# Small loads queued behind the diagonals, two sums of squares on VectorE, and the tail of one modulation block on TensorE

## The chip, the core and the metric

The kernel runs on one core of a Trainium2 chip. The core has TensorE (PE, with its weight loads shown apart as PEld), VectorE (DVE), ScalarE (ACT), GpSimd (POOL) and SyncE (SP), and sixteen DMA engines that they share. Each engine works through its own instructions strictly in order; between engines, semaphores make one wait for another. The metric is device time in microseconds (us) from launch to end. Before the change it is 2052.8 us, the median of three runs (2052.47 to 2053.01).

## What is computed

Three transformer layers, one sequence of 512 rows, width 1024, all in 32-bit floating point. The change lies in the beginning of the first layer:

```python
c_act = jax.nn.silu(c)
mod = jnp.einsum('bd,de->be', c_act, w_ada[l]) + b_ada[l]          # 6 x 1024 columns
sh1, sc1, g1, sh2, sc2, g2 = [m[:, None, :] for m in jnp.split(mod, N_ADA, axis=-1)]
h = rmsnorm(x, norm_mix_g[l]) * (1.0 + sc1) + sh1
proj = jnp.einsum('bsd,de->bse', h, w_in[l])
u_f, q, k, v = jnp.split(proj, split_cols, axis=-1)
q = rmsnorm(q.reshape(B, S, N_KV_HEADS, Q_PER_KV, HEAD_DIM), q_norm_g[l])
k = rmsnorm(k.reshape(B, S, N_KV_HEADS, HEAD_DIM), k_norm_g[l])
y_f = fourier_mix(u_f, w_fourier[l], b_fourier[l])
y_a = windowed_gqa(q, k, v, rel_bias, sink[l])                     # rel_bias: T5 bias table
mixed = jnp.einsum('bse,ed->bsd', jnp.concatenate([y_f, y_a], axis=-1), w_out[l])
x = x + g1 * mixed
```

A mixture of 16 experts follows in the same layer, then two more layers with other attention forms.

## The kernel before

**Phases.** `phase_a` makes everything quoted above; the expert phase and four more phases follow. The work is staged as one stream of 1 MB weight chunks (`wraw`, 128 x 2048 values), which SP loads in a fixed order; a chunk's load waits until its buffer is free. The first ten chunks take turns between a pool of three buffers and the two of `wp`; from then on there are the two buffers of `wp` alone, so a load is issued when the chunk two places earlier has been read.

**Modulation.** The 6144 columns of `mod` are worked in twelve blocks of 512, two chunks (halves) each. For a block, DVE adds up `acc[p, n] = sum over k of ca[p, k] * w[p, k, n]` in eight steps (`sums`, L656 and L658, for the first four blocks; `mod`, L612 and L614, for the others), and PE then sums over the partitions with a matrix of ones: into four columns (`columns`, L584) or, where the result is wanted as a row on all partitions (blocks 4, 5, 10, 11), as one 512-wide product (L619). Those four blocks start from a row of `b_ada`, which POOL loads into `acc` (L596) after clearing it (L594). The order of chunks is: block 2, block 0, first half of q, block 3, block 1, second half of q, block 4 (both halves), kv, block 5 (both halves), u (first), blocks 6 to 11 among u (second) and the attention.

**Start.** `load_x` brings the four row chunks of x. For each, ACT squares and sums (`ssq`, L444), `rstd` makes the reciprocal root on ACT and DVE, and POOL writes a diagonal matrix with it (`diags`, L694). PE multiplies x with the diagonals (`turn`, L674), which transposes and normalises in one go; `modulate` (L681 to L685) applies scale `a1` and shift `sh` and splits the result into a high and a low part, `hT_hi` and `hT_lo`. Weights are split likewise, `whi` on ACT (L403) and `wlo` on DVE (L404), and every product is three matmuls (`mm3`, L413 to L415).

**Then** come q (`proj_m`, into `qn`), kv (L736 copies the result out), the constants of the Fourier part (`fourier_mats`, L913), the sums of squares of q and k (`qss`, L741 to L743, which need both q and kv), their `rstd` over 40 columns, u (`pieces("u")`, `proj_s`), the scaled k and q (L767, L774) with their transposes (L777), the Fourier part, and attention in four blocks.

**Small loads** go through POOL's queue: the T5 table (`t5_table`: `c_t`, `tab`, then `t5scr`, which goes through DRAM and comes back as eight `bias` loads in `t5_bias`), `row_sink`, and `wf`, `c_cd`, `c_sd` for the Fourier part. Loads that are not pinned may be placed anywhere by the scheduler.

**Order.** A scheduler sets the order of each engine's instructions when the kernel is built, from data dependencies and its own estimates; an instruction given to `pin` keeps its place in program order among the pinned ones. What stands in a row on an engine is therefore fixed before the run.

Of the kernel before, what the change touches and what calls it, by code (L numbers as in the profile page):

```python
# [11 lines left out]
F32 = mybir.dt.float32  # L12
F32R = mybir.dt.float32r
BF16 = mybir.dt.bfloat16
# [3 lines left out]
OP = mybir.AluOpType  # L18
# [5 lines left out]
D = 1024  # L24
# [269 lines left out]
class Kernel:  # L294
# [262 lines left out]
    def phase_a(self, moe, pre):  # L557
        nc, tc, sp = self.nc, self.tc, self.sp
        with ExitStack() as es:
# [3 lines left out]
            p = self.pool(ea, "a_p")  # L563
# [5 lines left out]
            ones = pb.tile([128, 128], F32, name="ones")  # L569
# [12 lines left out]
            def columns(acc, pm, first=True, last=True):  # L582
                for j in range(4):
                    nc.tensor.matmul(pm[:, j:j + 1], acc[:, j * 128:j * 128 + 128], ones[:, :1],  # L584
                                     start=(j == 0 and first), stop=(j == 3 and last))
# [53 lines left out]
            pq = self.pool(e3, "a_q", side="right")  # L639
            pa = self.pool(e1, "a_ada", side="right")  # L640
# [2 lines left out]
            sh, a1, bg = (pa.tile([128, 8], F32, name=n) for n in ("sh", "a1", "bg"))  # L643
            nc.vector.scalar_tensor_tensor(bg, vc("ada", 8), 1.0, vc("mix", 0), op0=OP.add, op1=OP.mult)

            def sums(blk):
                acc = pb.tile([128, 512], F32, name="acc", bufs=2)
                for h in range(2):
                    w, _ = self.raw("ada")
                    if h == 1 and blk == 2:  # L650
                        self.load_x()
                    for k in range(4):
                        ck = ca[:, 4 * h + k:4 * h + k + 1]
                        wk = w[:, k * 512:(k + 1) * 512]
                        if h + k == 0:
                            nc.vector.tensor_scalar(acc, wk, ck, None, op0=OP.mult)  # L656
                        else:
                            nc.vector.scalar_tensor_tensor(acc, wk, ck, acc, op0=OP.mult, op1=OP.add)  # L658
                return acc

            def put(blk, pm):
                sl = slice(blk % 2 * 4, blk % 2 * 4 + 4)
                if blk < 2:
                    nc.vector.tensor_tensor(sh[:, sl], pm[:, :4], vc("ada", 4 * blk, 4), op=OP.add)
                else:
                    nc.vector.tensor_tensor(a1[:, sl], pm[:, :4], vc("mix", 4 * blk - 8, 4), op=OP.mult)
                    nc.vector.tensor_tensor(a1[:, sl], a1[:, sl], bg[:, sl], op=OP.add)

            diags = []

            def turn(k):
                pt = self.mm()
                for c in range(4):
                    nc.tensor.matmul(pt[:, c * 128:(c + 1) * 128], self.x[:, c, k * 128:(k + 1) * 128],  # L674
                                     diags[c], start=True, stop=True)
                return pt

            def modulate(k, pt):
                t = pa.tile([128, 512], F32, name="hx", bufs=2)
                if k % 2:  # L680
                    nc.scalar.activation(t, pt, AF.Identity, scale=a1[:, k:k + 1], bias=sh[:, k:k + 1])  # L681
                else:
                    nc.vector.tensor_scalar(t, pt, a1[:, k:k + 1], sh[:, k:k + 1], op0=OP.mult, op1=OP.add)
                nc.scalar.copy(hT[0][:, k], t)
                nc.vector.tensor_tensor(hT[1][:, k], t, hT[0][:, k].bitcast(F32), op=OP.subtract)  # L685

            acc = sums(2)
            pm = self.av()
            columns(acc, pm)
            put(2, pm)  # L690
            for c in range(4):
                rr = self.rstd(self.ssq(self.x[:, c]), 1, D)
                diags.append(pa.tile([128, 128], F32, name=f"diag{c}"))
                nc.gpsimd.tensor_scalar(diags[-1], self.ident, rr, -0.5, op0=OP.mult, op1=OP.mult)  # L694
            pts = [turn(k) for k in range(4)]
            scr = self.t5_table(pq)
            acc = sums(0)
            pm = self.av()
            columns(acc, pm)
            put(0, pm)  # L700
            for k in range(4):
                modulate(k, pts[k])

            def third(i):
                if i == 0:
                    pts[:] = [turn(k) for k in range(4, 7)]

            def second(i):
                if i == 0:
                    accs = [sums(3), sums(1)]  # L710
                    pm = self.mm()
                    for j in range(2):
                        columns(accs[j], pm[:, 4 * j:4 * j + 4], j == 0, j == 1)
                    put(3, pm)
                    put(1, pm[:, 4:8])
                    for k in range(4, 8):
                        modulate(k, pts[k - 4] if k < 7 else turn(k))
                fill(FILL[i], self.mm)
# [4 lines left out]
                        banks=[self.av] * 2 + [self.tp] * 2)  # L723
            e1.close()
            p = self.pool(ea, "a_p2")
            sink = self.row_load(p, "sink", 8)
            kv = p.tile([128, 4, 256], F32, name="kv")
            qz = p.tile([128, 4, 2, 512], F32, name="qz")
            nc.gpsimd.memset(qz[64:, :, 0, :], 0.0)
# [2 lines left out]
            with ExitStack() as e2:  # L732
# [6 lines left out]
                for c in range(4):  # L739
                    sq = self.nrm.tile([128, D], F32, name="xn", tag="xn")  # L740
# [6 lines left out]
                                               op0=OP.mult, op1=OP.mult)  # L747

                d = 0
                for j in range(2):  # L750
                    for w in self.pieces("u", 128):
                        ps = self.mm()
# [128 lines left out]
    def t5_table(self, tmp):  # L881

        nc = self.nc
        t5 = self.const_load(tmp, "t5", 33)
        tab = tmp.tile([33, 8], F32, name="tab")
        nc.vector.memset(tab, 1.0)
        nc.gpsimd.dma_start(tab[:32], self.ap["rel_bias"])
        ps = self.tp()
        self.pin(nc.tensor.matmul(ps[:8], tab, t5[:33], start=True, stop=True))
        v = tmp.tile([8, 512], F32, name="t5v")  # L890
        self.pin(nc.scalar.copy(v, ps[:8]))
        scr = self.dram.tile([8, 16, 512], F32, name="t5scr")
        self.pin(nc.gpsimd.dma_start(scr, v[:, None, :].to_broadcast([8, 16, 512])))
        return scr
# [9 lines left out]
    def fourier_mats(self, p, tmp):  # L904

        nc = self.nc
        wf = tmp.tile([64, 8, 64], F32, name="wf")
        nc.gpsimd.dma_start(wf, self.ap["w_fourier"].rearrange("g c d -> c g d"))
        mats = []
        for n in ("cd", "sd"):  # L910
            cd = self.const_load(tmp, n, 64)
            ps = self.tp()
            self.pin(nc.tensor.matmul(ps, cd[:64], wf.rearrange("p g d -> p (g d)"), start=True, stop=True))  # L913
            m = p.tile([128, 4, 128], F32, name="m_" + n)
            nc.gpsimd.memset(m, 0.0)
            p4 = ps.rearrange("p (j g d) -> p j g d", j=4, g=2)
            nc.scalar.copy(m[:64, :, :64], p4[:64, :, 0])
            nc.vector.tensor_copy(m[64:, :, 64:], p4[64:, :, 1])
            mats.append(m)
        return mats  # L920
# [1057 lines left out]
```

## Time and profile before

| | |
|---|---|
| median of three runs | 2052.8 us |
| the profiled execution, its own time | 2050.99 us |
| its span, first to last instruction | 2049.2 us |
| PE busy / DVE busy / ACT busy / POOL busy | 95% / 67% / 52% / 6% of the span |
| chain of work that ended last | PE 66%, DVE 10%, issue 6%, ACT 4% |
| phase A | about the first 245 us of the span |

The busy shares are averages over phases with different limits. In phase A the stretches of 20 us tell more: they show each engine's busy time, PE's granted clock and what the DMA engines moved.

### The profile page before, as it was taken

To read this page: it belongs to the slowest core of one execution; us is meant where nothing else is said; L and a number is where in the kernel's file an instruction comes from. 1 tells how busy PE (TensorE), PEld (TensorE's weight loads), DVE (VectorE), ACT (ScalarE), POOL (GpSimd) and SP (SyncE) were. 2 spreads that over 40 slices of the span, in tenths; PEclk is the share of its full clock that TensorE was granted. 3 is DMA by queue.
4 is the path that set the end of the run, shared out by engine and by line. 5 is a ranking of instruction groups with operands and counts; after the bars stand their busy time and mean duration, and the time that the engine had idled before them with its cause. 6 is when DMAs were issued, how large, how long until landed. Compare 5 with 4: busy or idle time off the path is not lost.

```text
span 2049.2 us, 24617 instructions
## 1 busy us (share of the span) xinstructions
PE 1939.1 (95%) x9147; PEld 1532.6 (75%) x9147; DVE 1363.5 (67%) x2294; ACT 1058.4 (52%) x1831; POOL 133.2 (6%) x132
## 2 busy tenths in 40 slices
PE   5999789999999998999999999999999989999998
PEld 4777567677676676877778888887887778888886
DVE  7885689999898998438665624554447775624554
ACT  3444377878777775346454423433345664423432
POOL 3004100000000201000110000002000020000001
PEclk9999889999999999999999999999999999999999
DMA  9635559999999983220222222222322032222221
GB/s 294 249 141 194 230 215 420 402 394 370 417 375 394 405 336 121 103 72 11 97 90 103 78 98 103 89 92 71 122 73 73 31 114 103 77 98 103 99 82 57
DMA packets 53805, 358.30 MB, mean 175 GB/s; under 512 B 6566, under 2 KB 7134, under 8 KB 13876
## 3 DMA queue, kind: packets, MB, share of 16 engines
q1 hardware_dynamic: 48148, 338.60, 43.1%
q0 software_dynamic: 5536, 18.12, 3.1%
q8 instruction: 72, 1.18, 0.2%
q14 instruction: 49, 0.40, 0.1%
HBM read 353.28 MB, written 4.46 MB: 175 GB/s over the span
## 4 chain that ended last, share of the span: by engine, by line
PE 66%; DVE 10%; issue 6%; ACT 4%; POOL 0%; DMA 0%; DVEq 0%; ACTq 0%; POOLq 0%
PE mm L413 12%; PE mm L414 12%; PE mm L415 12%; PE mm L281 11%; DVE wlo L281 5%; PE tp L413 2%; PE tp L414 2%; PE tp L415 2%; PE av L414 2%; PE av L415 2%; PE av L413 2%; ACT whi L281 2%; PE mm L1381 1%; PE tp L281 1%; PE av L281 1%
## 5 line engine op out<-in xcount | busy, mean ns | idle before, releaser
L404 DVE TENSOR_TENSOR wlo<-wraw,whi 128x1024 fp32r<-128x1024 f32 (+2 forms) x209 | 250.1, 1199 | 395.1 <-ACT whi L403 395.1
L281 DVE TENSOR_TENSOR wlo<-wraw,whi 128x1024 fp32r<-128x1024 f32 x336 | 392.7, 1217 | 31.2 <-ACT whi L281 28.7
L403 ACT CAST whi<-wraw 128x1024 fp32r<-128x1024 f32 (+2 forms) x209 | 214.2, 1029 | 326.4 <-PE mm L414 149.1
L413 PE MATMUL mm<-hT_hi,whi 128*128 128x512 f32 (+1 forms) x960 | 376.0, 393 | 0.2 <-DVE sba L1706 0.2
L415 PE MATMUL mm<-hT_hi,wlo 128*128 128x512 f32 (+1 forms) x960 | 373.5, 389 | 1.8 <-DVE wlo L404 1.8
L414 PE MATMUL mm<-hT_lo,whi 128*128 128x512 f32 (+1 forms) x960 | 374.3, 390 | 0.6 <-DVE hT_lo L419 0.6
L281 ACT CAST whi<-wraw 128x1024 fp32r<-128x1024 f32 x336 | 331.3, 1054 | 19.6 <-PE mm L281 17.4
L415 PEld LDWEIGHTS mm<-hT_hi,wlo 128*128 128x128 f32 x960 | 182.2, 190 | 43.2 <-DVE wlo L404 2.0
L413 PEld LDWEIGHTS mm<-hT_hi,whi 128*128 128x128 f32 x960 | 182.3, 190 | 41.3 <-ACT xn L742 0.8
L414 PEld LDWEIGHTS mm<-hT_lo,whi 128*128 128x128 f32 x960 | 182.1, 190 | 40.9 <-DVE hT_lo L419 1.4
L281 PE MATMUL mm<-whi,xs 128*128 128x512 f32 x448 | 186.6, 416 | 0.6 <-DVE xs L281 0.6
L281 PE MATMUL mm<-wlo,xs 128*128 128x512 f32 x448 | 181.0, 404 | 4.7 <-DVE wlo L281 4.7
L281 PEld LDWEIGHTS mm<-wlo,xs 128*128 128x128 f32 x448 | 85.4, 191 | 35.0 <-DVE wlo L281 16.5
L281 PEld LDWEIGHTS mm<-whi,xs 128*128 128x128 f32 x448 | 85.5, 191 | 21.4 <-ACT whi L281 1.9
L414 PE MATMUL mm<-wlo,hT_hi 128*128 128x512 f32 (+2 forms) x256 | 98.1, 385 | 1.2 <-DVE wlo L404 1.2
L413 PE MATMUL mm<-whi,hT_hi 128*128 128x512 f32 (+2 forms) x256 | 98.5, 388 | 0.8 <-ACT whi L403 0.8
L415 PE MATMUL mm<-whi,hT_lo 128*128 128x512 f32 (+2 forms) x256 | 97.3, 381 | 0.6 <-DVE hT_lo L419 0.6
L281 PE MATMUL mm<-whi,act 128*128 128x512 f32 x224 | 96.5, 431 | 0.0
L281 PE MATMUL mm<-wlo,act 128*128 128x512 f32 x224 | 90.4, 404 | 2.3 <-DVE wlo L281 2.3
L418 ACT CAST aT_hi<-cv 128x512 fp32r<-128x512 f32 x44 | 27.3, 621 | 116.9 <-DVE cv L1887 116.9
L1886 ACT ACTIVATE cv<-cv 128x512 f32<-128x512 f32 x44 | 27.8, 632 | 89.4 <-DVE cv L1883 89.4
L414 PE MATMUL av<-wlo,aT_hi 128*128 128x512 f32 x176 | 69.2, 393 | 0.0
(513 smaller groups left out, 3368.7 us busy)
## 6 DMA issues: line engine op xcount, KB each, us to landing
wraw<-in_wts SPq DMA_DIRECT2D x310, 1024.0 KB, 7.2
wraw<-in_wts SPq DMA_DIRECT2D x8, 768.0 KB, 4.2
x<-in_x SPq DMA_DIRECT2D x4, 512.0 KB, 12.3
out<-x SPq DMA_DIRECT2D x4, 512.0 KB, 2.6
wraw<-in_wts SPq DMA_DIRECT2D x2, 832.0 KB, 4.6
bias<-t5scr POOLq DMA_DIRECT2D x8, 192.0 KB, 9.5
hd<-xn POOLq DMA_DIRECT2D x3, 512.0 KB, 2.9
mod<-md POOLq DMA_DIRECT2D x1, 1024.0 KB, 10.5
```

What stands on the lines that cost most here:

```text
L281: ins = op(*a, **k)
L403: i1 = nc.scalar.copy(hi[:, :n], t[:, a:a + n])
L404: i2 = nc.vector.tensor_tensor(lo[:, :n], t[:, a:a + n], hi[:, :n].bitcast(F32), op=OP.subtract)
L413: mm(ps, a[0], b[0], start=start, stop=False)
L414: mm(ps, a[0], b[1], start=False, stop=False)
L415: mm(ps, a[1], b[0], start=False, stop=stop)
L418: self.nc.scalar.copy(hi, src)
L1381: nc.tensor.matmul(ps[:, :W], lhs[:, i * 128:(i + 1) * 128], rhs[:, :W], start=True, stop=True)
L1886: nc.scalar.activation(u[0], u[0], AF.Silu)
```

## The change

Four edits. (1) Loads: `c_t` and `tab` (now made after the second modulation block), `wf`, `c_cd`, `c_sd` and `row_sink` are pinned, and so are the four diagonals, so that these loads come after the diagonals in POOL's queue. (2) Chunks 1 and 3 of x are squared and summed on DVE with one tensor_tensor_reduce each; chunks 0 and 2 stay on ACT. (3) The last two of the eight steps of block 0 leave DVE: PE multiplies the chunk with the two columns of `ca` (one row of 512, in the bank `side`), ACT copies that row out, and four more one-column products add it to `pm`. (4) `t5_table` is called after `modulate` instead of before `sums(0)`.

```diff
-            def sums(blk):
+            def sums(blk, aside=None):
...
-                        if h + k == 0:
+                        if aside is not None and 4 * h + k > 5:
+                            nc.tensor.matmul(aside[:1], ck, wk, start=(k == 2), stop=(k == 3))
+                        elif h + k == 0:
                             nc.vector.tensor_scalar(acc, wk, ck, None, op0=OP.mult)
...
             for c in range(4):
-                rr = self.rstd(self.ssq(self.x[:, c]), 1, D)
+                if c % 2:
+                    ssq = sp.tile([128, 1], F32, name="ssq", tag="ssq")
+                    nc.vector.tensor_tensor_reduce(pa.tile([128, D], BF16, name="sq"), self.x[:, c], self.x[:, c], 1.0, 0.0,
+                                                   op0=OP.mult, op1=OP.add, accum_out=ssq)
+                else:
+                    ssq = self.ssq(self.x[:, c])
+                rr = self.rstd(ssq, 1, D)
                 diags.append(pa.tile([128, 128], F32, name=f"diag{c}"))
-                nc.gpsimd.tensor_scalar(diags[-1], self.ident, rr, -0.5, op0=OP.mult, op1=OP.mult)
+                self.pin(nc.gpsimd.tensor_scalar(diags[-1], self.ident, rr, -0.5, op0=OP.mult, op1=OP.mult))
             pts = [turn(k) for k in range(4)]
-            scr = self.t5_table(pq)
-            acc = sums(0)
+            side = self.tp()
+            acc = sums(0, side)
+            row = pa.tile([1, 512], F32, name="siderow")
+            nc.scalar.copy(row, side[:1])
             pm = self.av()
-            columns(acc, pm)
+            columns(acc, pm, True, False)
+            for j in range(4):
+                nc.tensor.matmul(pm[:, j:j + 1], row[:, j * 128:j * 128 + 128], ones[:1, :1], start=False, stop=(j == 3))
             put(0, pm)
             for k in range(4):
                 modulate(k, pts[k])
+            scr = self.t5_table(pq)
...
-            sink = self.row_load(p, "sink", 8)
+            sink = self.row_load(p, "sink", 8, pin=True)
...
-        t5 = self.const_load(tmp, "t5", 33)
+        t5 = tmp.tile([33, 512], F32, name="c_t5")
+        self.pin(nc.gpsimd.dma_start(t5, self.ap["t5"]))
...
-        nc.gpsimd.dma_start(tab[:32], self.ap["rel_bias"])
+        self.pin(nc.gpsimd.dma_start(tab[:32], self.ap["rel_bias"]))
...
-        nc.gpsimd.dma_start(wf, self.ap["w_fourier"].rearrange("g c d -> c g d"))
+        self.pin(nc.gpsimd.dma_start(wf, self.ap["w_fourier"].rearrange("g c d -> c g d")))
...
-            cd = self.const_load(tmp, n, 64)
+            cd = tmp.tile([64, 128], F32, name="c_" + n)
+            self.pin(nc.gpsimd.dma_start(cd, self.ap[n]))
```

The order of instructions changes well beyond these lines, up to the end of phase A; the rows of all later phases stand as they did.

POOL before, from its first work to the first attention loads (L694 are the diagonals, L594 and L596 clear `acc` and load its row for blocks 4 and 5):

```order
L570 MEMSET ones 128x128
L366 DMA c_t_230<-in_t 33x512
L887 DMA tab<-in_rel_bias 32x8
L357 DMA row_sink<-in_rows 128x8
L729 MEMSET qz 64x4x512
L730 MEMSET qz 64x4x512
L908 DMA wf<-in_w_fourier 64x8x64
L366 DMA c_cd<-in_cd 64x128
```

POOL now (L703 are the diagonals, L915 the bias loads):

```order
L703 TENSOR_SCALAR diag_210<-ident,rs_y 128x128
L899 DMA c_t_274<-in_t 33x512
L902 DMA tab<-in_rel_bias 32x8
L908 DMA t5scr<-t5v 128x1x512
L594 MEMSET acc 128x512 x2
L596 DMA acc<-in_rows 1x16x32
L357 DMA row_sink<-in_rows 128x8
L915 DMA bias<-t5scr 16x8x384 x8
L743 MEMSET qz 64x4x512
L744 MEMSET qz 64x4x512
L596 DMA acc<-in_rows 1x16x32
```

The eight bias loads stood ahead of both `acc` clears; now they stand behind them and behind the first `acc` row, and the second `acc` row stands behind the bias loads and two large clears.

DVE before, from the split of the kv weights (`L404 ... x2`) on; `L614` are the steps of block 5, four for each half:

```order
L404 TENSOR_TENSOR wlo<-wraw,whi 128x1024 x2
L614 SCALAR_TENSOR_TENSOR acc<-wraw,ca,acc 128x512 x6
L743 TENSOR_REDUCE qss<-xn 128x10
L614 SCALAR_TENSOR_TENSOR acc<-wraw,ca,acc 128x512 x2
L743 TENSOR_REDUCE qss<-xn 128x10
L404 TENSOR_TENSOR wlo<-wraw,whi 128x1024 x2
```

The same place now (L757 are the reductions, L781 the scaled k, L788 the scaled q, and the last line is the split of u's weights):

```order
L404 TENSOR_TENSOR wlo<-wraw,whi 128x1024 x2
L757 TENSOR_REDUCE qss<-xn 128x10 x4
L427 TENSOR_SCALAR rs_v<-qss,eps 128x40
L432 TENSOR_TENSOR rs_t<-rs_y 128x40
L433 TENSOR_TENSOR rs_t<-rs_t,rs_v 128x40
L434 SCALAR_TENSOR_TENSOR rs_y<-rs_t,rs_y 128x40
L781 TENSOR_TENSOR xn<-kv,rs_y 128x128 x2
L788 TENSOR_TENSOR qn<-qn,rs_y 128x512 x4
L614 SCALAR_TENSOR_TENSOR acc<-wraw,ca,acc 128x512 x8
L404 TENSOR_TENSOR wlo<-wraw,whi 128x1024 x2
```

All eight steps of block 5 moved behind the whole normalisation of q and k; on PE the product that closes block 5 (L619) still stands directly after the last kv matmul and ahead of everything of u.

PE now, at the place where block 0 ends (L657 is the moved work, L904 the T5 product, L677 the turn of x):

```order
L657 MATMUL tp<-wraw,ca 1x512 x2
L584 MATMUL av<-ones,acc 128x1 x4
L712 MATMUL av<-ones,siderow 128x1 x4
L904 MATMUL tp<-c_t_274,tab 8x512
L677 MATMUL mm<-diag_172,x 128x128
L677 MATMUL mm<-diag_185,x 128x128
```

The T5 product stood ahead of block 0's columns; now it stands behind them, directly ahead of the rest of the turn and the q matmuls.

## Rows read from the trace of the kernel before

**Rows 1.** Stretches: ten together (60-240), then one; busy, clock, DMA share, GB/s.

```profile
sum 180.00, PE 169.37 PEld 136.87 DVE 126.93 ACT 77.59 POOL 26.79; mean PE 16.94 PEld 13.69 DVE 12.69 ACT 7.76 POOL 2.68
240.00:260.00 20.00, 2.75 (x20) 2.26 (x19) 16.20 (x63) 6.86 (x12) 5.54 (x5) 0.58 0.77 311
```

**Rows 2.** The same columns, three stretches of the start.

```profile
5.00:8.00 3.00, 0.35 (x1) 0.06 (x1) 0.65 (x7) 0.74 (x1) 2.96 (x3) 1.00 0.98 250
11.00:15.00 4.00, 0.00 (x0) 0.00 (x0) 2.53 (x5) 0.00 (x0) 0.00 (x0) 1.00 1.03 281
17.00:20.00 3.00, 1.84 (x8) 1.78 (x8) 1.10 (x6) 2.88 (x7) 0.00 (x0) 1.00 1.06 434
```

**Rows 3.** Timeline: start, duration, engine, line, out<-in, count, idle before.

```profile
22.89 0.54 POOL L694 TENSOR_SCALAR diag<-ident,rs_y 128x128 f32<-128x128 f32 x1 [0.93 <-DVE rs_y L434]
23.23 5.48 DVE L658 SCALAR_TENSOR_TENSOR acc<-wraw,ca,acc 128x512 f32<-128x512 f32 x7
29.85 0.16 DVE L664 TENSOR_TENSOR sh<-av,col 128x4 f32<-128x4 f32 x1 [1.14 <-PE av L584]
30.78 1.22 DVE L404 TENSOR_TENSOR wlo<-wraw,whi 128x1024 fp32r<-128x1024 f32 x1
31.94 0.77 PE L413 MATMUL av<-whi,hT_hi 128*128 128x512 f32 x1
```

**Rows 4.** Timeline: the tensor_tensor_reduce of the attention, two widths.

```profile
130.14 0.41 DVE L799 CUSTOM_DVE_ANT_0 sc<-mm,bias 128x256 f32<-128x256 f32 x1
133.94 0.56 DVE L799 CUSTOM_DVE_ANT_0 sc<-mm,bias 128x384 f32<-128x384 f32 x1
```

**Rows 5.** DMA issues: queue, count, size, median us from issue to landing.

```profile
c_t<-in_t POOLq DMA_DIRECT2D x1, 66.0 KB, 2.6
c_cd<-in_cd POOLq DMA_DIRECT2D x1, 32.0 KB, 7.9
```

**Rows 6.** The clock: the stretch in which the q matmuls begin.

```profile
31.50:34.50 3.00, 3.00 (x10) 2.47 (x10) 3.00 (x5) 2.75 (x6) 0.00 (x0) 0.50 1.02 410
```

**Rows 7.** Bias loads and what they meet; the wraw issue is at 43.5.

```profile
37.74 4.20 POOL L900 DMA_DIRECT2D bias<-t5scr  x8 [8.70 <-DMA t5scr<-t5v]
47.54 0.52 POOL L594 MEMSET acc<- 128x512 f32 x1 [5.60 <-PE mm L584]
42.00:50.00 8.00, 7.56 (x45) 6.41 (x43) 7.85 (x14) 3.01 (x4) 1.99 (x4) 1.00 1.03 132
wraw<-in_wts SPq DMA_DIRECT2D x1, 1024.0 KB, 12.8
56.49 3.11 DVE L614 SCALAR_TENSOR_TENSOR acc<-wraw,ca,acc 128x512 f32<-128x512 f32 x4 [1.57 <-DMA acc<-in_rows]
66.02 0.62 PE L413 MATMUL mm<-whi,hT_hi 128*128 128x256 f32 x3 [0.76 <-ACT whi L403]
```

**Rows 8.** Timeline of PE and ACT around the end of the kv matmuls.

```profile
78.23 1.02 PE L619 MATMUL av<-acc,ones 128*128 128x512 f32 x2
81.09 0.50 PE L413 MATMUL mm<-hT_hi,whi 128*128 128x512 f32 x1
78.75 0.38 ACT L736 COPY kv<-mm 128x256 f32<-128x256 f32 x1
79.01 0.33 ACT L742 ACTIVATE xn<-kv 128x128 f32<-128x128 f32 x1
82.27 0.33 ACT L426 ACTIVATE rs_y<-qss,eps 128x40 f32<-128x40 f32 x1 [0.65 <-DVE qss L743]
```

**Rows 9.** Timeline of DVE, block 5 and the normalisation of q and k.

```profile
68.58 3.11 DVE L614 SCALAR_TENSOR_TENSOR acc<-wraw,ca,acc 128x512 f32<-128x512 f32 x4
81.41 0.82 DVE L743 TENSOR_REDUCE qss<-xn 128x10 f32<-128x640 f32 x1
87.37 0.68 DVE L774 TENSOR_TENSOR qn<-qn,rs_y 128x512 f32<-128x512 f32 x1
```

**Rows 10.** DMA issue: the weight chunk of u, issued at 71.72.

```profile
wraw<-in_wts SPq DMA_DIRECT2D x1, 1024.0 KB, 4.8
```

More of the change, by code (lines that the diff above doesn't have):

```diff
@@ L883, in t5_table @@
         nc = self.nc
-        t5 = self.const_load(tmp, "t5", 33)
+        t5 = tmp.tile([33, 512], F32, name="c_t5")
+        self.pin(nc.gpsimd.dma_start(t5, self.ap["t5"]))
         tab = tmp.tile([33, 8], F32, name="tab")
         nc.vector.memset(tab, 1.0)
-        nc.gpsimd.dma_start(tab[:32], self.ap["rel_bias"])
+        self.pin(nc.gpsimd.dma_start(tab[:32], self.ap["rel_bias"]))
         ps = self.tp()
-        self.pin(nc.tensor.matmul(ps[:8], tab, t5[:33], start=True, stop=True))
+        self.pin(nc.tensor.matmul(ps[:8], tab, t5, start=True, stop=True))
         v = tmp.tile([8, 512], F32, name="t5v")
@@ L907, in fourier_mats @@
         wf = tmp.tile([64, 8, 64], F32, name="wf")
-        nc.gpsimd.dma_start(wf, self.ap["w_fourier"].rearrange("g c d -> c g d"))
+        self.pin(nc.gpsimd.dma_start(wf, self.ap["w_fourier"].rearrange("g c d -> c g d")))
         mats = []
         for n in ("cd", "sd"):
-            cd = self.const_load(tmp, n, 64)
+            cd = tmp.tile([64, 128], F32, name="c_" + n)
+            self.pin(nc.gpsimd.dma_start(cd, self.ap[n]))
             ps = self.tp()
-            self.pin(nc.tensor.matmul(ps, cd[:64], wf.rearrange("p g d -> p (g d)"), start=True, stop=True))
+            self.pin(nc.tensor.matmul(ps, cd, wf.rearrange("p g d -> p (g d)"), start=True, stop=True))
             m = p.tile([128, 4, 128], F32, name="m_" + n)
```

## Prediction, made before the changed kernel ran

> **What bounds the kernel now.** I read the chain of waits first: it is mostly PE. Then the stretches of 20 us, to see where phase A is not PE alone. From 60 to 240 us PE is busy 169.4 of 180 us, so it idles 10.6 us in all, and after that it waits for the router, at a granted clock of 0.58 [rows 1]. Phase A from 60 us on is therefore a queue of PE work with small holes: what delays PE there delays the end, and what comes earlier helps only if weights and splits come earlier too. Then the timeline of the start, where PE waits for others: the last diagonal is written at 22.89, seven of block 0's eight steps run on DVE from 23.23 to 28.71, `sh` is there at 29.85, the first split of q's weights starts at 30.78, and the first q matmul at 31.94 [rows 3]. Last, DVE and ACT around 80 us, because the order of rows on DVE changes there.
>
> **The start (edits 1 to 4).** The small loads cost the big ones bandwidth: at 5 to 8 us the engines moved 250 GB/s, at 11 to 15 us 281, once the small ones are gone 434 [rows 2]. All of that charged to them is 3 x (1 - 250/434) + 4 x (1 - 281/434) = 1.3 + 1.4 = 2.7 us by which x could land earlier; the other end is zero. A square on DVE is not in the trace: the tensor_tensor_reduce takes 0.41 us for 256 columns and 0.56 for 384 [rows 4], so 0.56 + 5 x 0.145 = about 1.3 us for 1024, much like ACT's square; since DVE first has to finish block 2, and ACT's second square now waits behind the small ACT steps of DVE's first, I take the last diagonal 1 us earlier, not 2.7. Block 0 then has six steps in place of eight; one is 5.48 / 7 = 0.78 us [rows 3], so 1.6 us less, and `acc` is ready about 2.7 us earlier. PE adds two 512-wide products at 1.02 us each (L619, rows 8), ACT a small copy (estimate 0.4 to 0.6, from the 0.38 of rows 8), PE four more columns: `sh` comes about 1.8 us earlier. Of that, DVE gets less: ACT now makes its `hx` ahead of the first cast of q's weights, so the split of 30.78 moves by only about 0.7 us.
>
> On PE, the T5 product now stands between block 0's columns and the q matmuls, and PE cannot pass it. `c_t` and `tab` are issued behind the last diagonal, at about 22 us, and `tab` about 1.3 us after that. Before, `c_t` took 2.6 us on idle engines and `c_cd` 7.9 under load [rows 5]: `tab` lands between 26 and 31 us, PE comes to the product at about 27.9, when `sh` is ready, then 1.0 us for it and 1.3 for the turn. The first q matmul starts between 30.7 and 32.9, against 31.94 before: 1.2 us earlier to 0.9 later. I take **-0.5 us** for the whole start, near the loaded row, since at 22 us the engines are full of weights [rows 2]; ends -1.9 and +0.9.
>
> **The bias loads and kv.** These eight loads choke the engines: they are issued from 37.74 on; while they run, 42 to 50 us, the engines are fully busy and move 132 GB/s, and the weight chunk issued at 43.5 lands 12.8 us later [rows 7], 18.6 us after the first bias issue. That chunk, block 4, was not urgent. Now the bias loads wait on POOL behind two clears of `acc`, which wait for PE (47.54 before), then a row load and `row_sink` of 0.5 us each (4.20 / 8, rows 7): first bias issue at about 49.5. What is loaded then is kv, issued when block 4's first half is summed: DVE waited 1.57 us for its row behind the bias and ended at 59.6 [rows 7]; now at about 57. Landing 18.6 us after the first bias issue is 68.1; the old run shared its first microseconds with a q chunk, so perhaps 66.6. With 1.1 us for the cast, PE starts kv between 67.7 and 69.2, against 66.02: 1.7 to 3.2 later. If kv is not choked it starts with PE's own shift, -0.5. I take **+2.0 us** on top of the start for kv's beginning measured against before, that is, kv ends at 80 and not at 78.2; ends -0.5 and +3.2. In the sum the -0.5 of the start is thus swallowed.
>
> The Trainium skill ("DMA: Bandwidth & Descriptors", section "Anatomy of one DMA — SWDGE (gpsimd) path") fits a load from this queue as 2.0 us plus its bytes over 436 GB/s. By that a bias load would take an estimated 2.45 us, the eight would be down some 6 us after the first issue, and kv's start would not be touched: the sum would be 11.2 in place of 13.7. The trace does not agree for this pattern (132 GB/s); it is one of the rivals below.
>
> **The order on DVE, the main term.** Before, the eight steps of block 5 stood among kv's split and the four reductions, and were done when PE finished kv: PE went from the last kv matmul at 78.2 straight into L619 and was at u at 81.09, 2.9 us later [rows 8]. Now all eight steps stand behind the normalisation of q and k, and that needs the last row block of kv. DVE cannot pass it, and PE cannot pass L619. From the last kv matmul on: ACT copy and square 0.6 (78.75 to 79.34, rows 8); reduction 0.8 [rows 9]; two small ACT steps 0.6 (0.33 the first, rows 8); three 128x40 steps on DVE about 0.5 (0.16 for a tiny one, rows 3); two k products about 0.6; four q products 2.5 to 2.7 (0.68 each, rows 9); eight steps 2 x 3.11 = 6.2 [rows 9]; hand-overs 0.3. Sum 12.1 us in which PE has nothing it may run. Meanwhile u's chunk waits too: its buffer is that of block 5's first half, so it is issued 3.1 us before the end, at +9.0, lands 4.8 us later [rows 10], is cast by +14.9; PE comes out of L619 and the two Fourier products at +15.0. Both agree, so u starts **12.1 us** later. Ends 11 and 13.5: every member is a row in series, only hand-overs are open.
>
> **After it.** With two buffers, the next chunks follow at the pace of load and sum, each issued by what frees the buffer: block 6 waits for block 5's second half and u's split, and the second u chunk for block 6. The transposes of q, which stood partly among the second u matmuls, now all stand ahead of them. That adds 0 to 3 us. After 12 us of idling I also expect PE's clock at its lower level (1.2 GHz), as the q matmuls had it at 31.5 to 34.5 us (0.50) after a short idle time [rows 6]; 3 us at half rate cost 1.5, partly hidden where u waits for its load. Together **+2.0**, ends 0 and 4.5. Against that, DVE has done about 5 us of its work (the normalisation above) earlier, while PE waited, and PE's later holes, at most 10.6 us from 60 to 240 [rows 1], shrink where they were DVE's backlog: **-2.4**, ends 0 and -6.
>
> **Sum.** 2.0 + 12.1 + 2.0 - 2.4 = 13.7 us. On the profiled execution, 2050.99, that is 2064.7; the median of the runs stands 1.8 us above it (2052.8), so **2066.5 us**. All later phases have the same rows in the same order and only move.
>
> **Rivals.**
> *The bias loads don't choke kv.* If kv lands 4.8 us after its issue at 57, like u's chunk [rows 10], it is there before PE has finished q; the term of +2.0 becomes -0.5, the sum 11.2, the time 2064.0. For it: kv is issued later in the train of bias loads than block 4 was. Against it: 132 GB/s at a full share [rows 7]. Chance 0.1. It is what the Trainium skill's fit, in the section named above, would give.
> *Half of the stall is paid back.* DVE enters the u stage with less to do; if 7 of PE's 10.6 us of later holes close, and nothing is added behind u, the sum is 2.0 + 12.1 - 7 = 7, the time 2060. For it: from 60 to 240 us DVE is busy 127 of 180 us [rows 1], so it has room to catch up. Against it: the two-buffer chain of loads is late as well, and it paces DVE. Chance 0.13.
> *Not slower: PE catches up.* One mechanism: the stall at L619 only moves idle time that PE would have had later, and the start gives its full 2.7 us from the freed engines without the bias in kv's way. Price -2.7 + 12.1 - 10.6 = -1.2, so 2051.6. It decides from the point where more than 9 us of the later holes close; but these hold waits for ACT and for the router's first steps too, which do not shrink. Chance 0.05.
> *More is lost behind u.* The chain of loads, the lumped transposes and the low clock add 6 and nothing comes back: 2.0 + 12.1 + 6 = 20, the time 2073. Chance 0.1.
>
> **Chances and range.** The forecast (2062.5 to 2070.5) has 0.62. The range takes in the kv rival and half-way repayment, down to 2058.5, and reaches 2071 above; it leaves out about 0.18. A measurement of this kernel tells about 0.2%, 4.1 us, from no change: faster than 2048.7 needs the catch-up and luck, 0.03; between 2048.7 and 2056.9 the rest of it, 0.06; slower 0.91.
>
> **What would show it.** In the profile after: a wait of PE at L619 of 11 to 13 us with DVE's `acc` as releaser, at about 80 to 92 us; DVE idle before the reductions; u's first matmul at 94 to 98 us, not 81; the first q matmul within 1.2 us of 31.9; the bias loads between 49 and 66 us and a low GB/s there; kv's first matmul at 66 to 69 us, with a wait for ACT's cast, that for its load. The router's wait, between 240 and 260 us before [rows 1], moves by the whole sum. The prediction is wrong if PE has no long wait before u, if kv starts before 65, or if the attention begins less than 6 us later than before.

## The result and the profile after

The changed kernel takes 2072.8 us (median of four runs) against 2052.9 for the kernel before: a ratio of 1.0091, interval 1.0078 to 1.0103, slower by 19 us by the ratio, 19.9 by the medians. Run once more beside the experiments it was 1.0093 (1.0077 to 1.0109). The forecast was 2066.5, at most 2071: the direction and the main wait were right, the size was 6 us short.

The stretches of the profile after, of 20 or 40 us: length, busy time of TensorE, of its weight loads, of VectorE, ScalarE and POOL, granted clock, DMA share, GB/s. The last line sums the six stretches from 60 to 240.

```profile
60.00:80.00 20.00, 16.02 (x87) 14.06 (x86) 3.12 (x3) 6.29 (x10) 3.14 (x7) 0.83 0.70 207
80.00:100.00 20.00, 7.91 (x39) 5.16 (x38) 14.17 (x23) 6.36 (x15) 0.00 (x0) 0.73 0.27 100
100.00:120.00 20.00, 18.02 (x75) 13.31 (x73) 13.74 (x23) 4.66 (x13) 0.00 (x0) 0.84 0.56 198
...
sum 180.00, PE 155.47 PEld 123.52 DVE 109.74 ACT 69.68 POOL 26.79; mean PE 25.91 PEld 20.59 DVE 18.29 ACT 11.61 POOL 4.47
```

From 60 to 240 us TensorE now idles 24.5 us, not 10.6 [rows 1], and from 60 to 120 its clock is below 1 in every stretch. The list of TensorE's waits between 60 and 100 us (us in total, times, longest) says where the idle time is:

```profile
PE av L619 <- DVE acc L614: 12.1, 1, 12.1
PE mm L413 <- ACT whi L403: 4.0, 1, 4.0
```

One wait is for block 5's sum, the other for kv's first split. The timeline (start, duration, engine, line, out<-in, count, idle before) of POOL, TensorE and VectorE, in order of time:

```profile
50.20 4.38 POOL L915 DMA_DIRECT2D bias<-t5scr  x8
69.39 1.56 PE L413 MATMUL mm<-whi,hT_hi 128*128 128x256 f32 x4 [3.98 <-ACT whi L403]
80.45 0.82 DVE L757 TENSOR_REDUCE qss<-xn 128x10 f32<-128x640 f32 x1 [7.93 <-ACT xn L756]
87.28 2.49 DVE L788 TENSOR_TENSOR qn<-qn,rs_y 128x512 f32<-128x512 f32 x4
89.69 6.26 DVE L614 SCALAR_TENSOR_TENSOR acc<-wraw,ca,acc 128x512 f32<-128x512 f32 x8
96.00 2.07 PE L619 MATMUL av<-acc,ones 128*128 128x512 f32 x2 [12.09 <-DVE acc L614]
98.00 2.07 PE L929 MATMUL tp<-wf,c_cd 64*128 64x512 f32 x2
101.71 0.79 PE L413 MATMUL mm<-hT_hi,whi 128*128 128x512 f32 x1
```

VectorE stands idle for 7.93 us before the first reduction, with block 5's eight steps behind it in its order. The steps then run from 89.69, and TensorE, done with kv at 83.9, waits 12.09 us for them. Before, L619 stood at 78.23 and u at 81.09 [rows 8]; now they stand at 96.00 and 101.71.

The clock of four stretches (same columns as above): kv's first products, L619 to u, u's first products, and the start of q as in [rows 6].

```profile
69.00:75.00 6.00, 5.61 (x24) 5.35 (x25) 2.45 (x2) 2.26 (x4) 0.00 (x0) 0.50 0.54 195
96.00:101.50 5.50, 5.50 (x6) 1.66 (x6) 2.61 (x3) 2.84 (x4) 0.00 (x0) 0.50 0.69 261
101.50:106.00 4.50, 4.50 (x11) 3.42 (x11) 3.44 (x6) 0.37 (x1) 0.00 (x0) 0.50 0.68 237
31.50:34.50 3.00, 3.00 (x11) 2.56 (x10) 3.00 (x5) 2.46 (x5) 0.00 (x0) 0.50 0.57 227
```

Behind each of the two waits TensorE works at the lower level, 1.2 GHz, for some 6 us and some 10 us. Before, 66 to 80 and 80 to 95 us were at 1.00.

**The ledger.** Lining up the same TensorE instructions in both profiles gives how far each was late: q's first product +0.3; second half +0.15; kv's first product +3.4; kv's end +5.5; L619 +17.8; u's first product +20.6; u's later products +22.7; the second u chunk +24.9; from 180 us to the end +23.0 to +23.4. By cause: start 0.2, kv's late weights 3.3, kv at the lower clock 2.1, the stall 12.1, L619 to u at the lower clock 2.85, u at the lower clock 2.1, transposes ahead of the second u chunk 1.0, that chunk's first products at the lower clock 1.2, given back 1.7. These last two are stretches of 3.4 us at the lower clock, the first in the profile after and the second in the profile before, each without its like at that place in the other:

```profile
119.80:123.20 3.40, 2.92 (x9) 2.57 (x10) 3.15 (x4) 1.98 (x3) 0.00 (x0) 0.50 0.35 145
```

```profile
174.80:178.20 3.40, 3.40 (x12) 2.85 (x11) 0.74 (x3) 1.36 (x4) 0.86 (x1) 0.50 0.47 198
```

The profiled execution is the longest of its four (2074.35 against 2072.5 to 2072.9), and before's was on the short side (2050.99): 23.4 between two profiles, 19.9 between medians.

### The profile page after: what moved, and what is told of

The parts are those of the page before. It is cut to its first block, busy times and chain, and to the rows that moved or that the text cites. A ratio compares the mean times of both kernels' runs of the same rounds, so it can differ in the third digit from the quotient of the medians.

```text
span 2072.6 us, 24644 instructions
## 1 busy us (share of the span) xinstructions
PE 1952.2 (94%) x9159; PEld 1541.7 (74%) x9159; DVE 1364.0 (66%) x2296; ACT 1057.0 (51%) x1828; POOL 132.5 (6%) x132
## 4 chain that ended last, share of the span: by engine, by line
PE 68%; DVE 11%; ACT 4%; issue 3%; DVEq 0%; ACTq 0%
PE mm L413 12%; PE mm L415 12%; PE mm L414 12%; PE mm L281 12%; DVE wlo L281 5%; PE tp L413 2%; PE tp L414 2%; PE tp L415 2%; PE av L414 2%; PE av L415 2%; PE av L413 2%; ACT whi L281 2%; PE mm L1397 1%; PE tp L281 1%; PE av L281 1%
## 5 line engine op out<-in xcount | busy, mean ns | idle before, releaser
L404 DVE TENSOR_TENSOR wlo<-wraw,whi 128x1024 fp32r<-128x1024 f32 (+2 forms) x209 | 251.1, 1204 | 405.8 <-ACT whi L403 405.4
```

The source lines that it names most:

```text
L404: i2 = nc.vector.tensor_tensor(lo[:, :n], t[:, a:a + n], hi[:, :n].bitcast(F32), op=OP.subtract)
```

## The experiments

**Theory:** edit 4 moves the train of eight bias loads among the weight chunks and, with it, block 5 on VectorE; the train makes a chunk late, the order makes the stall, and each long wait is followed by TensorE at 1.2 GHz. **Rivals:** u's or kv's weights set the pace whatever the order; or edits 2 and 3, which do change the start, are to blame. Runs 1 to 4, 5 to 8 and 9 to 12 each shared a chip and its runs of before. These runs of before spread more (2051 to 2062 us) than the first ones, so each result is a ratio to them with its interval and a difference of medians, and traces decide what these can't.

**1. Only the order on VectorE put back.**

```diff
-                        nc.vector.scalar_tensor_tensor(acc, wk, ck, acc, op0=OP.mult, op1=OP.add)
+                        i = nc.vector.scalar_tensor_tensor(acc, wk, ck, acc, op0=OP.mult, op1=OP.add)
+                        if blk == 5:
+                            self.pin(i)
...
-                    nc.vector.tensor_reduce(ss[:, c], sq[:, :640].rearrange("p (h d) -> p h d", d=64), axis=AX.X, op=OP.add)
+                    self.pin(nc.vector.tensor_reduce(ss[:, c], sq[:, :640].rearrange("p (h d) -> p h d", d=64), axis=AX.X, op=OP.add))
```

> All four edits stay; only on VectorE block 5's eight steps (L614) and the four reductions (L757) are kept in the order in which the code calls them, so that block 5 comes ahead of the reductions again. Theory (the order on VectorE makes the stall): the wait of 12.09 us at L619 goes, and with it what came after it, the slow clock of L619 to u (2.85 and 2.07 us) and the lumped transposes (2.2 us); kv's late load (3.3 us) and its slow clock (2.1 us) stay. 2072.8 - 12.1 - 4.9 - 2.2 + 1.7 (the later gain that goes too) = about 2055.3, range 2053 to 2058. Rival (u's weights or kv's late start set the pace, the wait only moves): PE waits for u's split or load in place of L619, and the time stays above 2062.

Measured: 1.003 (1.0018 to 1.0042), +6.6 us by medians. TensorE goes from kv straight into block 5's product, but waits for kv, as the changed kernel does, and once more for the normalised q:

```profile
70.63 0.58 PE L413 MATMUL mm<-whi,hT_hi 128*128 128x256 f32 x1 [5.17 <-ACT whi L403]
...
84.28 1.02 PE L621 MATMUL av<-acc,ones 128*128 128x512 f32 x2
...
105.67 0.66 PE L793 MATMUL tp<-ident,qn 128*128 128x128 f32 x2 [4.36 <-DVE qn L790]
```

The stall is the order: with it went two thirds of the loss. My 2055.3, 2.4 us over before, was too low: normalising q, which the changed kernel does inside the stall, now comes late and costs 4.36 us at the transposes.

**2. TensorE kept busy in the stall.**

```diff
+                        for _ in range(12 if blk == 5 else 0):
+                            nc.tensor.matmul(ps, ones, g1[:, :512], start=True, stop=True)
                         nc.tensor.matmul(ps, ones, acc, start=True, stop=True)
```

> All four edits and the order of rows of the changed kernel stay, and so does the stall; TensorE is only given twelve products of no use (ones by g1, into the bank that L619 overwrites) right ahead of block 5's L619, so that it is not idle while it waits for VectorE. Theory (after the stall the clock is low because TensorE had been idle): L619 still starts at about 96, but the granted clock is 1.00 there, u starts at 98.9 in place of 101.7, and the end is 4.9 us earlier, 2.85 for L619 to L929 and 2.07 for u: 2068 (2066.5 to 2069.5). Rival (what is slow behind the stall is late weights and hand-overs, or the clock falls for another reason): 2072 to 2073, u at 101 or later.

TensorE's timeline, then stretches, with the same columns as above:

```profile
85.91 9.60 PE L620 MATMUL av<-g,ones 128*128 128x512 f32 x22
98.17 1.12 PE L621 MATMUL av<-acc,ones 128*128 128x512 f32 x2 [2.66 <-DVE acc L614]
...
101.14 0.50 PE L413 MATMUL mm<-hT_hi,whi 128*128 128x512 f32 x1
```

```profile
98.00:101.00 3.00, 2.83 (x6) 0.97 (x6) 0.24 (x2) 1.20 (x2) 0.00 (x0) 1.00 0.87 339
101.00:105.00 4.00, 3.71 (x15) 2.66 (x15) 3.69 (x6) 1.81 (x4) 0.00 (x0) 1.00 0.45 145
```

With TensorE busy, the way from block 5's product to u takes 2.97 us in place of 5.71, at a clock of 1.00, and u runs at full rate: the slow stretch behind the stall is the clock, and it goes when TensorE is kept busy. Lined up with the profile after, 4.2 us are won from L619 to u's later products. By the second u chunk 1.6 of them are lost again, 0.4 to a longer wait at the transposes and 1.2 to a stretch at the lower clock that is longer here (117.3 to 124.2 us, against 119.8 to 123.2). A further stretch at the lower clock, which the profile after does not have, takes 2.2 more:

```profile
182.20:192.40 10.20, 10.20 (x46) 9.51 (x46) 4.35 (x17) 2.68 (x3) 7.52 (x4) 0.50 0.42 153
```

The total is 1.0074 (1.0052 to 1.0096), +15.5 us. That is what the theory gave (2068 is 15 us over before), but the interval reaches the changed kernel's 1.0093 (1.0077 to 1.0109) as well: what the slow clock behind the stall costs at the end of the kernel is not shown.

**3. Edit 4 undone.**

```diff
             pts = [turn(k) for k in range(4)]
+            scr = self.t5_table(pq)
...
                 modulate(k, pts[k])
-            scr = self.t5_table(pq)
```

> Edits 1 to 3 stay, edit 4 is undone: the T5 table is called ahead of block 0's sums again. The bias loads then stand ahead of the clears of acc on POOL and block 5 ahead of the reductions on VectorE. Theory (edit 4 is what moves the bias loads and through them the order on VectorE): no wait at L619, kv starts at 66 to 67.5, and the time is 2053 to 2055: as before, but TensorE waits at the T5 product for its table, which lands at about 27, ahead of block 0's last columns, 1 to 2 us. Rival (the loads pinned in edit 1, behind which POOL clears qz and loads block 5's row late, are what costs): the time stays over 2060.

Measured: 1.0028 (1.0012 to 1.0044), +5.5 us (the theory gave 0 to +2). The order on VectorE is that of before and the stall is gone, so edit 4 is what flips it. But there is a new wait, which neither side expected:

```profile
26.65 0.59 PE L904 MATMUL tp<-c_t,tab 33*8 33x512 f32 x1 [2.57 <-DMA tab<-in_rel_bias]
...
57.91 1.41 PE L677 MATMUL mm<-diag,x 128*128 128x128 f32 x5 [7.09 <-DVE a L670]
```

The bias loads leave at 36.09, ahead of the last chunk of blocks 3 and 1 (37.72), which then takes 17.6 us. In before it left at 35.08, 2.7 us ahead of the train [rows 7], and took 7.4.

**4. The bias loads called after u.**

```diff
-            self.t5_bias(scr, bias)
...
+                self.t5_bias(scr, bias)
                 ptk = self.av()
```

> All four edits stay, but the eight bias loads are called behind u's products, not ahead of q's. VectorE then has block 5's steps mixed with the reductions, as before, and the bias loads leave after kv's weights. Theory (the bias loads choke kv's load, and their place moves block 5): kv starts at 66 to 66.5 at a granted clock of 1.00, no stall, and the time is 2051 to 2054. Rival (kv's load is late for another reason): kv still starts at 69 to 69.5 with half clock behind it, and the time is 5.4 us longer, 2056 to 2059.

Measured: 1.005 (1.0034 to 1.0066), +10.5 us, above both forecasts. kv starts on time, as the theory had it, though its clock is at 0.50 from 67.5 to 70.9 us; but nothing holds POOL back, so the train leaves at 56.35, level with kv's chunk, and holds up block 5's two chunks (16.4 and 13.5 us to landing); u's chunk, which needs the buffer of the first, leaves at 79.50 only:

```profile
66.06 0.39 PE L413 MATMUL mm<-whi,hT_hi 128*128 128x256 f32 x1 [1.51 <-ACT whi L403]
...
86.97 0.79 PE L413 MATMUL mm<-hT_hi,whi 128*128 128x512 f32 x1 [7.33 <-ACT whi L403]
```

**5. Edits 2 and 3 alone.** (The other edits are left out; no other line differs.)

> Only edits 2 and 3 (two squares on VectorE, the last two steps of block 0 on TensorE); the small loads and the T5 table are as before. The table is there early, so TensorE makes the T5 product right behind the turn at about 25, the table is stored by about 35 and the bias loads leave at 35 to 36, within 1 us of the chunk of block 1 that leaves when q's second split is done. Theory (what counts is on which side of that chunk the bias loads leave): if they are ahead of it, that chunk lands 6 us or more late, TensorE waits 5 to 7 us before the second half of q, and the time is before + 4 to + 7 us, although the start itself is 1 to 2 us earlier. Rival (an earlier start is a gain, and a chunk is not held up by loads of 192 KB): before - 2 to 0 us.

Measured: 1.0017 (1.0007 to 1.0026), +3.3 us: a little under the +4 to +7 of the theory, above the rival, and for another reason. The start is not earlier: the first q matmul is at 36.38, 4.4 us late, because TensorE is at the turn until 28.01 and only then takes the T5 product, the side products and the narrow rows. The late chunk (issued at 39.10, 1.2 us behind the train, 11.8 us to landing) costs a wait of only 1.34 us, not 5 to 7.

**6. Edits 1 and 4 alone.** (Squares and block 0's steps as before.)

> Only edits 1 and 4 (the small loads behind the diagonals, the T5 table called last); the squares and block 0's steps are as before. POOL and VectorE get the rows of the changed kernel around block 5. Theory (the moves alone make the loss, edits 2 and 3 have no part in it): a wait of 11.5 to 13 us at L619, kv late by 3 to 5 us, before + 18 to + 24 us. Rival (edits 2 and 3, which bring the start forward, set up the collision of the bias loads with kv): less than + 14 us.

Measured: 1.0081 (1.0064 to 1.0097), +17 us, a little under the range and above the rival's.

```profile
28.68 0.61 PE L413 MATMUL av<-whi,hT_hi 128*128 128x512 f32 x1 [0.73 <-ACT hT_hi L687]
...
66.95 1.55 PE L413 MATMUL mm<-whi,hT_hi 128*128 128x256 f32 x4 [3.85 <-ACT whi L403]
...
93.40 1.22 PE L619 MATMUL av<-acc,ones 128*128 128x512 f32 x1 [12.10 <-DVE acc L614]
```

Stall and late kv are those of the whole change. And q starts at 28.68, 3.3 us ahead of before, where the whole change has 32.26: edits 2 and 3 take away what edit 1 wins.

**7. As 1, with thin bias loads.** It leaves out the bias of seven heads of eight.

```diff
+            nc.gpsimd.memset(bias, 0.0)
...
-            self.pin(nc.gpsimd.dma_start(bias[16 * a:16 * a + 16],
+            self.pin(nc.gpsimd.dma_start(bias[16 * a:16 * a + 16, :1],
...
-                                        ap=[[511, 16], [8192, 8], [1, 384]])))
+                                        ap=[[511, 16], [8192, 1], [1, 384]])))
```

> As e1_block5_first (all four edits, block 5 pinned ahead of the reductions), but each of the eight bias loads takes one head of eight, 24 KB in place of 192, and the rest of bias is zero; the loads stand at the same place. Part of the computation is left out (the bias of seven heads). Theory (the bytes and rows of these loads are what makes kv late, and the slow clock follows from the wait): kv starts at 66 to 66.5 in place of 70.6, at a granted clock of 1.00, and the time is 6 us or more below e1_block5_first: before - 1 to + 3 us. Rival (kv is late for another reason, its chunk being issued late): kv starts at 69 or later, and the time is within 2 us of e1_block5_first.

Measured: 0.9998 (0.9989 to 1.0007). kv's timeline, the size and median time to landing of the bias loads, and the stretch of kv:

```profile
66.03 0.92 PE L413 MATMUL mm<-whi,hT_hi 128*128 128x256 f32 x3
```

```profile
bias<-t5scr POOLq DMA_DIRECT2D x8, 24.0 KB, 1.9
```

```profile
66.00:72.00 6.00, 5.67 (x46) 5.23 (x45) 4.86 (x6) 1.93 (x3) 0.00 (x0) 1.00 0.30 98
```

No wait for kv, clock 1.00, and 6.7 us less than in run 1 (+6.6 against -0.1): the size of the train, bytes and rows together, is what makes kv late, and kv's slow clock followed from that wait. The order (13.3 us, from +19.9 to +6.6) and the size of the train (6.7) are together, by medians, about the whole loss.

**8. The whole change, with the clears and rows of `acc` kept behind the bias loads.**

```diff
-                        nc.gpsimd.memset(acc, 0.0)
+                        self.pin(nc.gpsimd.memset(acc, 0.0))
                         src = self.ap["rows"]
-                        nc.gpsimd.dma_start(acc[:1], bass.AP(tensor=src.tensor,
+                        self.pin(nc.gpsimd.dma_start(acc[:1], bass.AP(tensor=src.tensor,
...
```

> All four edits stay; the clears of acc and its row loads (L594, L596) are kept in program order too, so that on POOL the eight bias loads stand ahead of them, as before the change. The order on VectorE is then that of before, block 5 ahead of the reductions. The T5 table lands at about 43.7, so the bias loads leave then and run to about 60, over the two chunks of block 4 (issued at about 44 and 47), as before. Theory (the place of the bias loads among the chunks decides both losses): no wait at L619, kv starts at 66 to 67.5, and the time is that of before, -1.5 to +2 us. Rival (the bias loads, now 6 us later than before, hold up block 4 and with it kv's issue): kv starts at 69 to 70 at half clock, but no stall: before + 5 to + 8 us.

Measured: 1.0036 (1.0025 to 1.0046), +7.0 us: the time of the rival, though the wait stands ahead of kv and not at it. VectorE has before's order again and the stall is gone, but the train leaves at 43.76, and the second chunk of block 4, issued at 47.13, takes 14.8 us. TensorE waits for that block's sum, and kv starts at 73.69:

```profile
70.98 2.07 PE L619 MATMUL mm<-acc,ones 128*128 128x512 f32 x2 [6.93 <-DVE acc L614]
```

**9. Of edit 1 the loads of `sink`, `wf`, `cd`, `sd` and the diagonals; no other edit.** `c_t` and `tab` leave at the start, and the T5 table is made where it was before.

> Of edit 1 only the diagonals and the loads of sink, wf, cd and sd are kept in order behind the diagonals; c_t and tab leave at the start and the T5 table is called ahead of block 0, as before; no edit 2, 3 or 4. Theory (freeing the engines for x is the one gain in the change, and the bias loads must leave behind block 1's chunk): the last diagonal is written at about 20 and not 22.9, the first q matmul starts at 28.7 to 29.7 and not 31.9, the bias loads leave at about 35, 2 us behind that chunk, nothing else moves, and the end is 1 to 3 us ahead of before (ratio 0.9985 to 0.9995). Rival (what is won at the start is lost again, since kv's or u's weights come no earlier): q starts early, kv or u waits for its chunk, and the time is that of before within 0.5 us. A second rival: the bias loads overtake the chunk, as in e5_two_three: before + 3 us or more.

Measured: **0.9979 (0.9970 to 0.9988)**, 2051.5 against 2056.0 us: faster than both kernels, and by more than the 1 to 3 us expected. The last diagonal is written at 20.23, q and the train start early, and kv does not wait longer than in [rows 7]:

```profile
20.23 0.54 POOL L703 TENSOR_SCALAR diag<-ident,rs_y 128x128 f32<-128x128 f32 x1 [1.03 <-DVE rs_y L434]
...
34.39 4.30 POOL L909 DMA_DIRECT2D bias<-t5scr  x8 [8.34 <-DMA t5scr<-t5v]
```

```profile
29.53 0.77 PE L413 MATMUL av<-whi,hT_hi 128*128 128x512 f32 x1
...
63.36 0.87 PE L413 MATMUL mm<-whi,hT_hi 128*128 128x256 f32 x4 [0.76 <-ACT whi L403]
```

The train leaves 2 us behind the last chunk of blocks 3 and 1 (32.41), as in before. Every TensorE instruction from q to 92 us is 2.4 to 3.0 us earlier than in the profile of before. Behind that this profile loses its lead again (see the clock, below), and at 256 us it is 0.4 us behind: the gain at the end rests on the times of the runs alone.

**10. The changed kernel again.** The same file.

> The changed kernel once more, for its ratio to before on the same chip as the other runs of this call, and for its waits in a second profile. If kv's late load and the stall are properties of the program: again a wait of 12.0 to 12.2 us at L619 and of 3.5 to 5 us ahead of kv, ratio 1.008 to 1.010. If kv's delay depends on the chip or the run, its wait differs by over 2 us from 3.98.

The waits come back, 4.06 us for kv and 12.10 at L619, as does the ratio: 1.0093 (1.0077 to 1.0109).

**11. Run 9 with edit 3.** (The side products, the row and its four columns come in; nothing else.)

> e9_loads_only plus edit 3 (the last two steps of block 0 on TensorE). Theory (at that place TensorE, not VectorE, is the late one: it is still at the turn, and then has two side products and eight narrow rows more): the side products start when the turn ends, about 25, sh is ready no earlier than in e9_loads_only, more of the turn is left over for behind it, and the first q matmul is 1 to 3 us later than there; if that also brings the bias loads level with block 1's chunk, 3 us more at the second half of q. Time 1 to 6 us over e9_loads_only. Rival (two steps less on VectorE are 1.5 us less on the path): the first q matmul and the end are 1 to 1.5 us ahead of e9_loads_only.

Measured: 0.9992 (0.9983 to 1.0001), 2.4 us over run 9. The side products start at 25.49, when the turn ends, and fourteen products of the turn are left for behind `sh`:

```profile
25.49 1.88 PE L657 MATMUL tp<-wraw,ca 128*1 128x512 f32 x4
...
28.29 1.05 PE L713 MATMUL av<-ones,siderow 1*128 1x1 f32 x8
30.40 3.05 PE L677 MATMUL mm<-diag,x 128*128 128x128 f32 x14 [1.06 <-ACT hx L684]
33.10 1.20 PE L413 MATMUL av<-whi,hT_hi 128*128 128x512 f32 x2
```

q starts at 33.10, 3.6 us behind run 9: edit 3 puts work on the engine that is late. The train leaves at 35.42, level with the last chunk of blocks 3 and 1 (35.62), which I had thought might cost 3 us; the chunk lands after 7.8 us and nobody waits for it.

**12. Run 9 with edit 2.** (Squares of chunks 1 and 3 on VectorE.)

> e9_loads_only plus edit 2 (the squares of chunks 1 and 3 on VectorE). Theory (the diagonals wait for x, not for the squares, and VectorE has block 2 to finish first): the last diagonal is no earlier than in e9_loads_only (within 0.4 us), block 0's eight steps start no earlier, and the time is that of e9_loads_only within 1 us. Rival (the squares on ScalarE hold up the diagonals): the last diagonal 0.7 us earlier or more, and q with it.

Measured: 0.9993 (0.9983 to 1.0002), 1.9 us over run 9 by medians, where I expected at most 1, with intervals that touch. The last diagonal is at 20.10 (run 9: 20.23), q at 28.88 (29.53): as expected, no gain on the diagonals. Whether edit 2 costs anything stays open.

**The train and the chunk behind it**, all from traces:

| kernel | train leaves | chunk behind it, issued | to landing, us | TensorE's wait for it, us |
|---|---|---|---|---|
| before | 37.74 | block 4, 43.54 | 12.8 | none of its own |
| run 9 | 34.39 | block 4, 40.88 | 13.0 | none of its own |
| run 11 | 35.42 | last of blocks 3 and 1, 35.62 | 7.8 | none of its own |
| run 5 | 37.94 | last of blocks 3 and 1, 39.10 | 11.8 | 1.34 |
| run 3 | 36.09 | last of blocks 3 and 1, 37.72 | 17.6 | 7.09 |
| run 8 | 43.76 | block 4, second, 47.13 | 14.8 | 6.93 |
| after | 50.20 | kv, 57.54 | 10.7 | 3.98 |
| run 4 | 56.35 | block 5, 59.80 | 16.4 | 7.33 (at u) |

The chunk behind the train is 10 to 18 us under way in each of them but run 11, where it is issued only 0.2 us behind. Nobody waits for it there, and where the train leaves some 6 us ahead of block 4's two chunks, which have that much slack.

## Why the prediction was right and wrong

- **The order on VectorE: right.** 12.1 us forecast, 12.09 measured; run 1 removes it with the order alone.
- **The bias loads and kv: right mechanism, under-sized.** +2.0 taken, ends -0.5 and +3.2; measured 3.4. They left at 50.20 (forecast 49.5), and kv's chunk landed at 68.27 (forecast 66.6 to 68.1). The rival that kv is not held up falls with run 7.
- **The clock: the term that failed.** I put 1.5 us, "partly hidden", for one stretch behind the stall and none for kv. Measured against before: 2.1 in kv, 2.85 from L619 to u, 2.1 in u and 1.2 in the second u chunk, 8.2 in all. The rows were there: [rows 6] shows 0.50, after two short waits of TensorE. I had not asked what stands in the 6 to 10 us behind each wait: dense matmuls, which at half rate cost half of what they cover.
- **The start: right within its ends, wrong reasons.** Forecast -0.5 (-1.9 to +0.9), measured +0.3. `tab` landed at 27.06, in time; the diagonals came 2.7 us earlier, the upper end, all by edit 1 (runs 9 and 12). Against that, I charged edit 3 with its own products only. Runs 5 and 11 show that they queue behind the turn on a late TensorE, and the turn's rest behind them: `sh` came 0.8 us earlier, not 1.8, and q not at all.
- **Behind u: low.** +2.0 in all; the transposes took 1.0 and the clock, counted above, 6.1.
- **Given back: right size, wrong cause.** -2.4 forecast, -1.7 measured between 167 and 183 us. It is not VectorE's backlog but a stretch of low clock in before that the profile after does not have there. The two rivals by which 7 to 10 us came back are ruled out.
- **The sum.** 13.7 forecast, 23.2 in the ledger and 19.9 between medians. The time of "more is lost behind u" (2073, chance 0.1) came out, in part by luck: behind the stall 7.1 were lost and not 6, but 1.7 came back, and kv was late by more than that rival had. Without the clock's 8.2 the ledger would end at about 15; that is arithmetic only, since run 2 shows the clock's cost up to u and not at the end.

## What to carry to other kernels

In this kernel a slow train of small loads cost nothing only where it left just behind the chunk that is needed next, or level with it, and ahead of one that is not; an edit that moves the train by a few microseconds picks another victim, so list what is issued within the 10 us behind it, in every variant. Look at the order on each engine after any edit, since one moved call can put eight urgent steps behind a wait for something else. And a wait of TensorE is to be priced together with the slow clock of the dense work behind it, as far as the runs go: up to the next stage, not to the end.

## What the runs showed of the hardware

**A queue that at times does not share.** Packets by queue in the profile after, one stretch of 1 us with the train and kv's chunk both outstanding (59.5 to 60.5 us), then one from 62 to 63 (packets, MB, share of 16 engines):

```profile
q0 software_dynamic: 52, 0.16, 117.2%
```

```profile
q1 hardware_dynamic: 20, 0.16, 102.5%
q0 software_dynamic: 17, 0.02, 16.1%
```

kv's chunk was issued at 57.54 on the hardware queue, and 2 to 3 us later only packets of the software queue ran. The Trainium skill ("DMA: Bandwidth & Descriptors", section "Queues, rings and completion order") says that each engine takes turns between its queues packet by packet; here the measurement shows one queue served until the train was nearly through. It is not always so: in run 5 the chunk was issued 1.2 us behind the train, not 7, and both queues were served, as from 45 to 46 us:

```profile
q1 hardware_dynamic: 22, 0.18, 80.2%
q0 software_dynamic: 17, 0.03, 17.0%
```

What decides between the two stays open.

**Clock.** The level does not follow a wait of a given length. In before, waits of 1.25 and 0.85 us among the transposes were followed by a clock of 1.00; in run 9 the same two places, with 1.41 and 0.81, by 0.50. In before itself a wait of 2.15 us, ending at 130.61, was followed by 1.00, and one of 1.42 us, ending at 51.39, by 0.50. The stretches are 97 to 103, 131 to 135 and 52 to 55 of before, then 94 to 100 of run 9:

```profile
97.00:103.00 6.00, 6.00 (x29) 4.92 (x29) 5.50 (x7) 1.56 (x3) 0.00 (x0) 1.00 0.91 333
131.00:135.00 4.00, 4.00 (x16) 2.80 (x15) 3.79 (x20) 0.33 (x1) 0.00 (x0) 1.00 0.00 0
52.00:55.00 3.00, 3.00 (x8) 2.32 (x7) 2.08 (x4) 1.92 (x3) 0.00 (x0) 0.50 0.94 331
```

```profile
94.00:100.00 6.00, 5.68 (x16) 4.50 (x17) 5.47 (x8) 2.13 (x4) 0.00 (x0) 0.50 0.87 303
```

Run 9 lost there all of its 2.7 us against that profile. Such steps of 2 to 3 us come and go between profiles of this kernel; that they also make the spread of single runs is likely, not shown.

**POOL beside VectorE.** While VectorE squared a chunk (17.82 to 19.03 in the profile after), POOL's second diagonal took 1.40 us of the pair's 1.90; in run 9, with that square on ScalarE, it took 0.38.

```profile
17.37 1.90 POOL L703 TENSOR_SCALAR diag<-ident,rs_y 128x128 f32<-128x128 f32 x2 [16.42 <-DVE rs_y L434]
```

```profile
17.82 1.21 DVE L697 CUSTOM_DVE_ANT_0 sq<-x 128x1024 bf16<-128x1024 f32 x1
```

The Trainium skill ("Advanced Engine Details and Errata", section "GPSIMD Details") says that POOL conflicts with VectorE instructions that have two inputs in SBUF; the square has, and the rows agree. In run 12, with the square on VectorE, it is 1.40 us again: against run 9 the second and third diagonals are done 0.6 us later, and the fourth only 0.1 us earlier.
